# Where SBUF tiles begin: one rule for all of them in place of a table of offsets for the split weights

## The chip, the cores and the metric

The kernel runs on one core of one Trainium2 chip. The time is that of one execution on the device in microseconds (us); three executions of the kernel before gave 3103.0, 3103.5 and 3106.6 us, with a median of 3103.5 us.

## The reference

The reference is a small model in float32 on 256 tokens of width 2048: an RG-LRU/mLSTM layer, an SSD layer, a block that mixes an S5, a gated-linear-attention and a differential-attention branch, and a gated feed-forward block, each with a root-mean-square norm and a residual. Nearly all of its arithmetic is in products of the activations with weight matrices:

```python
def rmsnorm(x, w):
    xf = x.astype(jnp.float32)
    y = xf * lax.rsqrt(jnp.mean(xf * xf, axis=-1, keepdims=True) + EPS)
    return (y * w.astype(jnp.float32)).astype(x.dtype)
...
    u = x @ w_in            # lru_mlstm_layer and ssd_layer: 2048 x 8192 and 2048 x 10304
...
    return y @ w_out        # 4096 x 2048
```

The other weights of that kind are `w_in_2`, `w_out_2`, `ffn_w_up_2` (2048 x 11008), `ffn_w_down_2` and a few smaller ones. The result is wanted in float32, and the matrices are used once each.

## The kernel before

Activations stand with features on the 128 partitions and the 256 tokens along the free axis, two feature blocks to a tile: a tile `x`, `a`, `h` or `b` is 128 x 2 x 256 float32, 2048 bytes in each partition. A weight matrix is cut into blocks of 128 x 128. They come from HBM in one long stream, in the order in which they are used: SP's queue loads eight blocks at a time into a tile `w` (three buffers), and `_split_part` makes of every four blocks (a **part**) two tiles: `wh`, the weights rounded to float32r by ScalarE (L249), and `wl`, the remainder, by VectorE (L250). There are six buffers of each. `ahead` runs this five parts ahead of the products.

`prod` (L280 to L282) multiplies one block with one 128 x 256 activation block in three matmuls: `wh` with the high half of the activations, `wh` with their low half, and `wl` with the high half. They add up in a PSUM tile `pm`. Before each matmul TensorE loads its weights anew, so the stream is a chain of pairs: a weight load (128 columns, 512 bytes in each partition) and a matmul (256 columns, 1024 bytes in each partition). The load for the next matmul runs while the present one streams its activations. The trace has 24,144 such pairs; the program has 8048 blocks, and 3 x 8048 = 24,144. In the main pattern a part gives twelve matmuls, L280, L281, L282 four times.

Everything else (convolutions, scans, norms, gates, the small matmuls of the branches) runs beside the stream on VectorE, ScalarE and GpSimd, or is put into the stream in short pieces by `pump`.

SBUF is given out by pools in the order in which they are opened: constants (`cst`), the weight stream (`wp`: `w`, `wh`, `wl`), activations that live long (`xp`), scratch (`tmp`), and then the pools of each stage. Every pool begins where the one before ends. In the kernel before, the sizes of the small constant tiles so set where all that follows begins. `wpart` gives each `wh` and `wl` tile 96 bytes more than it needs (2144 in place of 2048) and lets the weights begin some bytes into it:

```python
WH_OFF, WL_OFF = (0, 0, 0, 0, 16, 16), (8, 8, 4, 4, 24, 12)
...
    def wpart(self, tag, o):

        t = self.wp.tile([P, SP * P + 24], F32R, name=self.nm(tag), tag=tag, bufs=6)
        return t[:, o // 4:o // 4 + SP * P].rearrange("p (b c) -> p b c", b=SP)
...
        h = self.wpart("wh", WH_OFF[i % 6])
        l = self.wpart("wl", WL_OFF[i % 6])
```

The part's number modulo 6 picks the offset.

Of the kernel before, what the change touches and what calls it, by code (L numbers as in the profile page):

```python
# [9 lines left out]
F32 = mybir.dt.float32  # L10
F32R = mybir.dt.float32r
# [8 lines left out]
P = 128  # L20
T = 256
D = 2048
KD = D // P
EPS = 1e-6
CH = 8

# [4 lines left out]
SP = 4  # L31

WH_OFF, WL_OFF = (0, 0, 0, 0, 16, 16), (8, 8, 4, 4, 24, 12)
HEADS = 4
# [62 lines left out]
NPAR = _o  # L97
# [9 lines left out]
NCON = _o  # L107
# [44 lines left out]
class Builder:  # L152
    def __init__(self, nc, tc, d, dbg, ctx):
        self.nc, self.tc, self.d, self.dbg = nc, tc, d, dbg
        self.ctx = ctx
        pool = lambda **k: ctx.enter_context(tc.tile_pool(**k))
        self.cst = pool(name="cst", bufs=1)
        self.wp = pool(name="wp", bufs=1)
        self.xp = pool(name="xp", bufs=1)
        self.tp = pool(name="tmp", bufs=1)  # L160
        self.pm = pool(name="pm", bufs=1, space=PSUM)
        self.ps = pool(name="ps", bufs=1, space=PSUM)
        self.dr = pool(name="dr", bufs=1, space=DRAM)
        self.uid = 0
        self.side = []

        self.plan = []
        at = {}
        for name, n in _plan():
            assert n % CH == 0, name  # L170
            for _ in range(n // CH):
                self.plan.append((name, at.get(name, 0)))
                at[name] = at.get(name, 0) + 1
        self.w_dma = 0
        self.w_split = 0
        self.w_pos = 0
        self.raw, self.hl = {}, {}
# [10 lines left out]
    def close(self, cm):  # L188
        cm.__exit__(None, None, None)

    def act(self, shape=(P, 2, T), dt=F32, pool=None):
# [44 lines left out]

    def wpart(self, tag, o):

        t = self.wp.tile([P, SP * P + 24], F32R, name=self.nm(tag), tag=tag, bufs=6)
        return t[:, o // 4:o // 4 + SP * P].rearrange("p (b c) -> p b c", b=SP)  # L240

    def _split_part(self, i):
        nc = self.nc
        c, b = divmod(i * SP, CH)
        w = self.raw[c][:, b:b + SP]
        h = self.wpart("wh", WH_OFF[i % 6])
        l = self.wpart("wl", WL_OFF[i % 6])
        for s in [slice(0, SP)] if i else [slice(0, SP // 2), slice(SP // 2, SP)]:
# [191 lines left out]
    def run(self):  # L440
        nc, d = self.nc, self.d
        self.params = self.cst.tile([P, NPAR], F32, name="params")
        self.consts = self.cst.tile([P, NCON], F32, name="consts")

# [72 lines left out]
    def layer_one(self):  # L517
# [14 lines left out]

        cmw = self.cst.tile([P, 80], F32, name="cmw")
        nc.vector.tensor_scalar(cmw, self.par("conv_m_w", 0, 80), 0.5, None, op0=ALU.mult)
# [9 lines left out]

        sp = self.cst.tile([P, 16], F32, name="lru_sp")
        hb = self.cst.tile([P, 32], F32, name="lru_hb")
        lam = self.par("lru_lam", 0, 16)
# [279 lines left out]
    def layer_two(self):  # L827
# [8 lines left out]
        self.st, scm = self.open("ssd")  # L836
        cw = st.tile([P, 240], F32, name="ocw")
        nc.vector.tensor_scalar(cw, self.par("o_conv_w", 0, 240), 0.5, None, op0=ALU.mult)
# [51 lines left out]

        fw = st.tile([P, 16], F32, name="fw")
        nc.vector.tensor_tensor(fw, self.par("final_norm", 0, 16), self.par("norm_mix", 0, 16), op=ALU.mult)
# [617 lines left out]
    def diff(self, qd, kd, vd, oh, ol):  # L1510
# [11 lines left out]
        nc.scalar.dma_start(ali, d["consts2"][:, 384:].rearrange("p (h k) -> p h k", h=4))  # L1522
        lam = self.st.tile([P, 1], F32, name="lam")
        V.tensor_tensor(lam, e[:, 0:1], e[:, 1:2], op=ALU.subtract)
# [37 lines left out]
    def ffn(self):  # L1562
# [5 lines left out]
        self.stage = (st, "a", 34)  # L1568
        gw = st.tile([P, 4, 43], F32, name="gw")
        for k in range(3):  # L1570
# [169 lines left out]
```

## Time and profile before

| | |
|---|---|
| median of three runs | 3103.5 us |
| the profiled execution's own time | 3105.49 us |
| its span, first to last instruction | 3103.7 us |
| TensorE (matmul) busy | 3080.1 us, 99% |
| TensorE weight loads busy | 3029.1 us, 98% |
| VectorE busy | 2301.3 us, 74% |
| ScalarE busy | 1748.7 us, 56% |
| GpSimd busy | 90.5 us, 3% |
| DMA | 556 MB, 179 GB/s on average |
| mean granted TensorE clock | 0.997 of full speed |

A matmul's row in the trace lasts some 282 ns although the next one begins after some 118 ns: matmuls are pipelined. What one costs in the stream is therefore the distance from its start to the next one's start, here called its **pace**. It is read from the timeline (starts of neighbouring rows) or from the windows view (length of a stretch divided by the count of matmuls that lie in it). The timeline shows starts to 0.01 us; the trace holds them in nanoseconds, and means over many matmuls below are taken from those.

### The profile page before, as it was taken

Reading aid. Unit: us, or ns where it says so; the run is one execution under the profiler, and the core shown is the slowest. Engines: PE = TensorE matmul, PEld = TensorE weight load, DVE = VectorE, ACT = ScalarE, POOL = GpSimd, SP = SyncE. Lnnn points to the kernel's source line nnn. Section 1 sums busy time; section 2 is a strip of 40 time slices with the busy share of each in tenths; the row PEclk is TensorE's granted clock in tenths of the full one; section 3 lists DMA queues with packets and bytes.
Section 4 is the critical chain, followed back from the end, with each engine's and each line's share of the span. In section 5 each row is a group of like instructions: output and inputs, shape, how many; then the busy total and the mean of one; then the engine's idle time right before and its main releaser. Section 6 shows DMA issues by size and latency. Waiting matters only on the chain.

```text
span 3103.7 us, 66894 instructions
## 1 busy us (share of the span) xinstructions
PE 3080.1 (99%) x26310; PEld 3029.1 (98%) x26310; DVE 2301.3 (74%) x4693; ACT 1748.7 (56%) x3303; POOL 90.5 (3%) x123
## 2 busy tenths in 40 slices
PE   8999999999999999999999999999999999999998
PEld 8999999999999999999999998999999999999998
DVE  8787766669888876778888786666677777567764
ACT  6666544556666555564555554555555555455554
POOL 1000000010000000020000000000000000000000
PEclk9999999999999999999999999999999999999999
DMA  6565545656565555565454554556556565655654
GB/s 233 182 184 161 178 159 184 186 178 217 185 191 175 168 179 180 193 200 178 153 154 152 165 170 149 160 162 203 186 184 187 184 186 188 185 184 186 188 184 150
DMA packets 153933, 556.30 MB, mean 179 GB/s; under 512 B 17392, under 2 KB 18544, under 8 KB 152592
## 3 DMA queue, kind: packets, MB, share of 16 engines
q1 hardware_dynamic: 148752, 534.89, 54.9%
q0 software_dynamic: 3104, 14.75, 1.3%
q8 instruction: 206, 3.38, 0.4%
q10 hardware_dynamic: 1760, 2.38, 0.2%
q14 instruction: 111, 0.91, 0.1%
HBM read 547.69 MB, written 4.26 MB: 178 GB/s over the span
## 4 chain that ended last, share of the span: by engine, by line
PE 99%; DVE 1%; DMA 0%; ACT 0%; issue 0%; SPq 0%; DVEq 0%
PE pm L280 31%; PE pm L282 31%; PE pm L281 31%; PE ps L1004 1%; PE ps L1306 0%; PE ps L1344 0%; PE ps L1465 0%; PE ps L369 0%; PE ps L1291 0%; PE ps L1236 0%; PE ps L798 0%; PE ps L973 0%; PE ps L682 0%; PE ps L683 0%; DMA w<-w_first 0%; PE ps L1440 0%
## 5 line engine op out<-in xcount | busy, mean ns | idle before, releaser
L249 ACT CAST wh<-w 128x512 fp32r<-128x512 f32 (+1 forms) x2013 | 1239.6, 622 | 1212.6 <-PE pm L281 1028.5
L250 DVE TENSOR_TENSOR wl<-w,wh 128x512 fp32r<-128x512 f32 (+1 forms) x2013 | 1392.5, 698 | 635.8 <-ACT wh L249 611.2
L280 PE MATMUL pm<-x,wh 128*128 128x256 f32 x5504 | 1559.0, 283 | 6.1 <-ACT wh L249 6.1
L282 PE MATMUL pm<-x,wl 128*128 128x256 f32 x5504 | 1553.3, 283 | 3.3 <-DVE q L426 3.1
L281 PE MATMUL pm<-x,wh 128*128 128x256 f32 x5504 | 1549.7, 282 | 0.5 <-DVE x L487 0.4
L280 PEld LDWEIGHTS pm<-x,wh 128*128 128x128 f32 x5504 | 1040.5, 189 | 15.0 <-issue 7.8
L282 PEld LDWEIGHTS pm<-x,wl 128*128 128x128 f32 x5504 | 1039.4, 189 | 7.2 <-DVE q L426 3.3
L281 PEld LDWEIGHTS pm<-x,wh 128*128 128x128 f32 x5504 | 1039.9, 189 | 3.2 <-issue 1.9
L280 PE MATMUL pm<-a,wh 128*128 128x256 f32 x1712 | 483.1, 282 | 0.5 <-ACT wh L249 0.5
L282 PE MATMUL pm<-a,wl 128*128 128x256 f32 x1712 | 483.0, 282 | 0.0
L281 PE MATMUL pm<-a,wh 128*128 128x256 f32 x1712 | 481.9, 282 | 0.3 <-DVE a L333 0.3
L280 PEld LDWEIGHTS pm<-a,wh 128*128 128x128 f32 x1712 | 323.4, 189 | 0.9 <-ACT wh L249 0.7
L281 PEld LDWEIGHTS pm<-a,wh 128*128 128x128 f32 x1712 | 322.6, 188 | 0.6 <-DVE a L333 0.5
L282 PEld LDWEIGHTS pm<-a,wl 128*128 128x128 f32 x1712 | 322.6, 188 | 0.2
L280 PE MATMUL pm<-h,wh 128*128 128x256 f32 x576 | 163.6, 284 | 0.6 <-DVE t L1090 0.6
L281 PE MATMUL pm<-h,wh 128*128 128x256 f32 x576 | 162.5, 282 | 0.0
L282 PE MATMUL pm<-h,wl 128*128 128x256 f32 x576 | 161.8, 281 | 0.0
L280 PEld LDWEIGHTS pm<-h,wh 128*128 128x128 f32 x576 | 108.5, 188 | 4.6 <-issue 3.1
L281 PEld LDWEIGHTS pm<-h,wh 128*128 128x128 f32 x576 | 108.7, 189 | 0.8 <-issue 0.8
L282 PEld LDWEIGHTS pm<-h,wl 128*128 128x128 f32 x576 | 108.5, 189 | 0.0
L417 DVE SCALAR_TENSOR_TENSOR a<-t,ocw,a 128x255 f32<-128x255 f32 (+1 forms) x144 | 64.6, 477 | 20.2 <-ACT a L415 20.1
L282 PE MATMUL pm<-b,wl 128*128 128x256 f32 x256 | 72.1, 282 | 0.0
(430 smaller groups left out, 2411.7 us busy)
## 6 DMA issues: line engine op xcount, KB each, us to landing
w<-w_up SPq DMA_DIRECT2D x172, 512.0 KB, 3.5
w<-w_w_in_u SPq DMA_DIRECT2D x114, 512.0 KB, 3.6
w<-w_o_in SPq DMA_DIRECT2D x98, 512.0 KB, 3.9
w<-w_w_in_g SPq DMA_DIRECT2D x96, 512.0 KB, 3.5
w<-w_down SPq DMA_DIRECT2D x86, 512.0 KB, 3.5
w<-w_e_in_z SPq DMA_DIRECT2D x64, 512.0 KB, 3.5
w<-w_e_out SPq DMA_DIRECT2D x64, 512.0 KB, 3.5
w<-w_o_z SPq DMA_DIRECT2D x64, 512.0 KB, 3.5
```

The lines of the kernel that those rows point to most:

```text
L249: nc.scalar.copy(h[:, s], w[:, s])
L250: nc.vector.tensor_tensor(l[:, s], w[:, s], h[:, s].bitcast(F32), op=ALU.subtract)
L280: nc.tensor.matmul(o, h, xh(k), start=k == 0, stop=False)
L281: nc.tensor.matmul(o, h, xl(k), start=False, stop=False)
L282: nc.tensor.matmul(o, l, xh(k), start=False, stop=k == KT - 1)
L417: nc.vector.scalar_tensor_tensor(dst[:, j:], u[:, :T - j], ws[taps - 1 - j], dst[:, j:], op0=ALU.mult, op1=ALU.add)
L1004: nc.tensor.matmul(o, xdt[s][:, 64 * ee:64 * ee + 64], r, start=s == 0, stop=s == 1, tile_position=(0, 64 * e))
```

## The change

The table of offsets and `wpart` go. `wh` and `wl` become plain tiles of 2048 bytes. A helper `line` rounds the odd-sized tiles (`params`, `consts`, `cmw`, `lru_sp`, `lru_hb`, `ocw`, `fw`, `lam`, `gw`) up to a multiple of 128 bytes, and two small pools of 64 bytes, `gap1` and `gap2`, stand before and behind the weight stream's pool.

```diff
--- before.py
+++ after.py
@@ -22,6 +22,7 @@
 D = 2048
 KD = D // P
 EPS = 1e-6
+LINE = 128
 CH = 8
 
 
@@ -29,8 +30,6 @@
 
 
 SP = 4
-
-WH_OFF, WL_OFF = (0, 0, 0, 0, 16, 16), (8, 8, 4, 4, 24, 12)
 HEADS = 4
 
 L1_ORDER = [("m", 0), ("l", 0), ("m", 1), ("q", 0), ("l", 1), ("l", 2), ("q", 1), ("m", 2), ("l", 3), ("l", 4), ("q", 2), ("m", 3), ("l", 5), ("l", 6), ("q", 3), ("l", 7)]
@@ -155,7 +154,10 @@
         self.ctx = ctx
         pool = lambda **k: ctx.enter_context(tc.tile_pool(**k))
         self.cst = pool(name="cst", bufs=1)
+
+        pool(name="gap1", bufs=1).tile([P, LINE // 8], F32, name="gap1")
         self.wp = pool(name="wp", bufs=1)
+        pool(name="gap2", bufs=1).tile([P, LINE // 8], F32, name="gap2")
         self.xp = pool(name="xp", bufs=1)
         self.tp = pool(name="tmp", bufs=1)
         self.pm = pool(name="pm", bufs=1, space=PSUM)
@@ -188,6 +190,14 @@
     def close(self, cm):
         cm.__exit__(None, None, None)
 
+    def line(self, shape, name, pool):
+
+        n = math.prod(shape[1:])
+        t = pool.tile([P, -(-n // (LINE // 4)) * (LINE // 4)], F32, name=name)[:, 0:n]
+        if len(shape) == 3:
+            t = t.rearrange("p (a b) -> p a b", a=shape[1])
+        return t
+
     def act(self, shape=(P, 2, T), dt=F32, pool=None):
 
         pool, tag, n = pool or self.stage
@@ -234,17 +244,12 @@
             self.nc.sync.dma_start(w[:, s], src[:, s])
         self.raw[i] = w
 
-    def wpart(self, tag, o):
-
-        t = self.wp.tile([P, SP * P + 24], F32R, name=self.nm(tag), tag=tag, bufs=6)
-        return t[:, o // 4:o // 4 + SP * P].rearrange("p (b c) -> p b c", b=SP)
-
     def _split_part(self, i):
         nc = self.nc
         c, b = divmod(i * SP, CH)
         w = self.raw[c][:, b:b + SP]
-        h = self.wpart("wh", WH_OFF[i % 6])
-        l = self.wpart("wl", WL_OFF[i % 6])
+        h = self.wp.tile([P, SP, P], F32R, name=self.nm("wh"), tag="wh", bufs=6)
+        l = self.wp.tile([P, SP, P], F32R, name=self.nm("wl"), tag="wl", bufs=6)
         for s in [slice(0, SP)] if i else [slice(0, SP // 2), slice(SP // 2, SP)]:
             nc.scalar.copy(h[:, s], w[:, s])
             nc.vector.tensor_tensor(l[:, s], w[:, s], h[:, s].bitcast(F32), op=ALU.subtract)
@@ -439,8 +444,8 @@
 
     def run(self):
         nc, d = self.nc, self.d
-        self.params = self.cst.tile([P, NPAR], F32, name="params")
-        self.consts = self.cst.tile([P, NCON], F32, name="consts")
+        self.params = self.line([P, NPAR], "params", self.cst)
+        self.consts = self.line([P, NCON], "consts", self.cst)
 
         st, self.start = self.open("start")
         x0 = st.tile([P, KD + 2 * T], F32, name="x0")
@@ -530,7 +535,7 @@
         nc.scalar.mul(rhalf, rstd, 0.5)
 
 
-        cmw = self.cst.tile([P, 80], F32, name="cmw")
+        cmw = self.line([P, 80], "cmw", self.cst)
         nc.vector.tensor_scalar(cmw, self.par("conv_m_w", 0, 80), 0.5, None, op0=ALU.mult)
         assert POFF["conv_m_b"] == POFF["conv_m_w"] + 64
         self.close(self.start)
@@ -542,8 +547,8 @@
         big = st.tile([P, 384], F32, name="big3")
         nc.scalar.dma_start(big, d["consts2"][:, 0:384])
 
-        sp = self.cst.tile([P, 16], F32, name="lru_sp")
-        hb = self.cst.tile([P, 32], F32, name="lru_hb")
+        sp = self.line([P, 16], "lru_sp", self.cst)
+        hb = self.line([P, 32], "lru_hb", self.cst)
         lam = self.par("lru_lam", 0, 16)
         u, s, q = self.small([P, 16]), self.small([P, 16]), self.small([P, 16])
         nc.scalar.activation(u, lam, AF.Abs)
@@ -834,7 +839,7 @@
         st, cm = self.open("two")
         self.stage = (st, "a", 28)
         self.st, scm = self.open("ssd")
-        cw = st.tile([P, 240], F32, name="ocw")
+        cw = self.line([P, 240], "ocw", st)
         nc.vector.tensor_scalar(cw, self.par("o_conv_w", 0, 240), 0.5, None, op0=ALU.mult)
         assert POFF["o_conv_b"] == POFF["o_conv_w"] + 192
 
@@ -888,7 +893,7 @@
 
 
 
-        fw = st.tile([P, 16], F32, name="fw")
+        fw = self.line([P, 16], "fw", st)
         nc.vector.tensor_tensor(fw, self.par("final_norm", 0, 16), self.par("norm_mix", 0, 16), op=ALU.mult)
         self.acc, self.acc2 = [], []
         self.xh, self.xl = [], []
@@ -1520,7 +1525,7 @@
         nc.scalar.activation(e, p, AF.Exp)
         ali = self.st.tile([P, 4, T], F32, name="alibi")
         nc.scalar.dma_start(ali, d["consts2"][:, 384:].rearrange("p (h k) -> p h k", h=4))
-        lam = self.st.tile([P, 1], F32, name="lam")
+        lam = self.line([P, 1], "lam", self.st)
         V.tensor_tensor(lam, e[:, 0:1], e[:, 1:2], op=ALU.subtract)
         V.tensor_scalar(lam, lam, LAMBDA_INIT, None, op0=ALU.add)
         scale = float(np.float32(128 ** -0.5))
@@ -1566,7 +1571,7 @@
 
         st, cm = self.open("ffn")
         self.stage = (st, "a", 34)
-        gw = st.tile([P, 4, 43], F32, name="gw")
+        gw = self.line([P, 4, 43], "gw", st)
         for k in range(3):
             nc.vector.tensor_scalar(gw[:, k], self.par("ffn_conv_w", 86 * k + 43, 43), 0.5, None, op0=ALU.mult)
         nc.vector.tensor_scalar(gw[:, 3], self.par("ffn_conv_b", 43, 43), 0.5, None, op0=ALU.mult)
```

No instruction is added, removed or moved: on each of the five engines the built program has the same instructions in the same order, with the same waits, and every tile keeps its number of buffers. What differs is where tiles begin. From the two built programs, in bytes within a partition:

| tiles | before | after |
|---|---|---|
| `wh` (6 buffers, with offset) | 0, 16, 32, 48, 64, 80 or 96 past a multiple of 128 | 64 past, all |
| `wl` (6 buffers, with offset) | 4, 8, 12, 36, 40, 68, 88, 104 or 120 past, never a multiple of 16 | 64 past, all |
| `w` | 96 past | 64 past |
| activations that the stream's matmuls read (`x`, `a`, `h`, `b`) | 96 past (87% of the matmuls) or 32 past | 0, all |
| `params`, `consts`, scratch, other stage tiles | 0, 32, 64 or 96 past | 0 |
| the S5 branch's tiles `s5bc` to `s5yx` | 0 | 32 past |

One more quantity is used below. The **distance** is the start of the activations that a matmul reads, less the start of the weights that are loaded meanwhile for the next matmul, modulo 512. (A weight block is 512 bytes and an activation block 1024, so all blocks of one part and one tile pool share a distance.) Before, parts come in 27 pairs of distances, one for `wh` and one for `wl`, which lies 60 to 72 bytes below it, modulo 512. After, both have the same distance in a part: 64 for 68.2% of the stream's matmuls, 192 for 20.7%, 448 for 8.7% and 320 for 2.4%.

## Rows read from the trace of the kernel before

**Rows 1.** The page: busy time, granted clock, and the chain that ended last

```profile
PE 3080.1 (99%) x26310; PEld 3029.1 (98%) x26310; DVE 2301.3 (74%) x4693; ACT 1748.7 (56%) x3303; POOL 90.5 (3%) x123
...
PEclk9999999999999999999999999999999999999999
...
PE 99%; DVE 1%; DMA 0%; ACT 0%; issue 0%; SPq 0%; DVEq 0%
PE pm L280 31%; PE pm L282 31%; PE pm L281 31%; PE ps L1004 1%; PE ps L1306 0%; PE ps L1344 0%; PE ps L1465 0%; PE ps L369 0%; PE ps L1291 0%; PE ps L1236 0%; PE ps L798 0%; PE ps L973 0%; PE ps L682 0%; PE ps L683 0%; DMA w<-w_first 0%; PE ps L1440 0%
```

**Rows 2.** The page's groups: line, tiles, count, busy us, mean ns, idle before

```profile
L249 ACT CAST wh<-w 128x512 fp32r<-128x512 f32 (+1 forms) x2013 | 1239.6, 622 | 1212.6 <-PE pm L281 1028.5
L250 DVE TENSOR_TENSOR wl<-w,wh 128x512 fp32r<-128x512 f32 (+1 forms) x2013 | 1392.5, 698 | 635.8 <-ACT wh L249 611.2
L280 PE MATMUL pm<-x,wh 128*128 128x256 f32 x5504 | 1559.0, 283 | 6.1 <-ACT wh L249 6.1
...
L280 PE MATMUL pm<-a,wh 128*128 128x256 f32 x1712 | 483.1, 282 | 0.5 <-ACT wh L249 0.5
...
L280 PE MATMUL pm<-h,wh 128*128 128x256 f32 x576 | 163.6, 284 | 0.6 <-DVE t L1090 0.6
...
L282 PE MATMUL pm<-b,wl 128*128 128x256 f32 x256 | 72.1, 282 | 0.0
```

**Rows 3.** Windows of uninterrupted stream: stretch, length, PE busy (matmuls), clock, DMA

```profile
2100.00:2140.00 40.00, 40.00 (x335) 1.00 0.65 213
...
2700.00:2960.00 260.00, 260.00 (x2197) 1.00 0.60 187
3020.00:3080.00 60.00, 60.00 (x509) 1.00 0.58 176
```

**Rows 4.** Four transposes of 128 columns in a row: timeline, then durations by line

```profile
732.61 0.60 PE L973 MATMUL ps<-consts,a 128*128 128x128 f32 x4
...
L973 PE MATMUL ps<-consts,a x64: 270/273/276, 732.6 to 1013.2; 128*128 128x128 f32 x64
```

**Rows 5.** Timeline, distance 64 for wh: the first part and the last

```profile
2139.99 0.28 PE L282 MATMUL pm<-h,wl 128*128 128x256 f32 x1
2140.10 0.28 PE L280 MATMUL pm<-h,wh 128*128 128x256 f32 x1
2140.22 0.28 PE L281 MATMUL pm<-h,wh 128*128 128x256 f32 x1
...
2141.40 0.28 PE L282 MATMUL pm<-h,wl 128*128 128x256 f32 x1
...
3081.86 0.28 PE L282 MATMUL pm<-a,wl 128*128 128x256 f32 x1
...
3083.27 0.28 PE L282 MATMUL pm<-a,wl 128*128 128x256 f32 x1
```

**Rows 6.** Timeline, distances 192 and 448 for wh: one part each

```profile
1128.14 0.28 PE L282 MATMUL pm<-a,wl 128*128 128x256 f32 x1
...
1129.56 0.28 PE L282 MATMUL pm<-a,wl 128*128 128x256 f32 x1
...
1996.79 0.28 PE L282 MATMUL pm<-x,wl 128*128 128x256 f32 x1
...
1998.21 0.28 PE L282 MATMUL pm<-x,wl 128*128 128x256 f32 x1
```

**Rows 7.** Timeline, distances 352 for wh and 284 for wl: one part

```profile
37.31 0.28 PE L282 MATMUL pm<-x,wl 128*128 128x256 f32 x1
...
38.77 0.28 PE L282 MATMUL pm<-x,wl 128*128 128x256 f32 x1
```

**Rows 8.** By line: durations in ns (least, median, most) of the two splitting operations

```profile
L249 ACT CAST wh<-w x2013: 388/621/740, 5.1 to 3080.6; 128x512 fp32r<-128x512 f32 x182, 128x256 fp32r<-128x256 f32 x1
...
L250 DVE TENSOR_TENSOR wl<-w,wh x2013: 411/692/1280, 5.5 to 3081.3; 128x512 fp32r<-128x512 f32 x182, 128x256 fp32r<-128x256 f32 x1
```

## The prediction

> **What bounds the kernel now.** The page comes first. TensorE is busy 99% of the span with matmuls and 98% with weight loads, the clock was granted in full in nearly every slice, and 99% of the chain that ended last is TensorE's own work, 93% of it the three lines of the weight stream [rows 1]. So the next question is not who waits for whom but what one matmul of the stream costs. The groups give the count: 5504 + 1712 + 576 + 256 = 8048 matmuls on each of L280, L281 and L282 (a group with the same count stands for each line), 24,144 in all, and almost no idle time before them, 6.1 us at most [rows 2]. The windows give the pace: 40.00 us / 335 = 119.4 ns, 260.00 / 2197 = 118.3, 60.00 / 509 = 117.9 [rows 3]. Over the 23,706 starts in the timeline that follow directly on one another (under 200 ns apart), the mean is 118.6 ns. 24,144 x 118.6 = 2863 us of the 3103.7 us span; the other 240 us are the small matmuls, the start and the end. A change of 1 ns in the pace is worth 24.1 us, 0.8% of the time, and 0.2% (6.2 us, about what a measurement of this kernel can tell from no change) is 0.26 ns.
>
> Is 118.6 ns near a floor? Four transposes of 128 columns take 0.60 us; without the last one's own 273 ns that is (600 - 273) / 3 = 109 ns for each pair of a weight load and a short matmul [rows 4]. The stream's pairs load as many weights and take 9.6 ns more, so up to 24,144 x 9.6 = 232 us could depend on how the two reads of SBUF meet.
>
> **That the pace depends on addresses** can be read from the trace of before, since the old table puts the weights at many distances from the activations. Take a part's twelve matmuls, from the start of the matmul before its first to the start of its last. With distances 352 (wh) and 284 (wl), the part in the rows takes 38.77 - 37.31 = 1.46 us, 121.7 ns each; all 111 such parts have a mean of 121.0 ns and a standard deviation of 0.2 [rows 7]. With distance 64 for wh and 504 or 508 for wl, the first part takes 2141.40 - 2139.99 = 1.41 us and the last 3083.27 - 3081.86 = 1.41 us, 117.5 ns each; all 46 have a mean of 117.9 and a deviation of under 0.2 [rows 5]. So what repeats is the pair of distances, not the stage: the 46 parts lie in three stages and read tiles h, b and a. Of the 1738 undisturbed parts, the means of the 27 pairs lie between 117.4 and 121.0.
>
> The Trainium skill speaks against this: "TensorE: Matmul & The Clock Gate", in Part 2, step 1, says that loading the next weights doesn't take read bandwidth from the running matmul, as there are two read ports, and "SBUF — State Buffer", in Who interferes with whom, says that PE never waits on anyone. By that rule the 121.0 and 117.9 ns should be one number, and the change would be worth nothing. The trace doesn't agree, but the rule has a milder form that is a rival below.
>
> **The change, part by part.**
>
> *Instructions.* None is added, removed or moved, no wait is new, and the number of buffers is the same. So every term but the pace is zero, if durations elsewhere don't follow alignment. For ScalarE's and VectorE's splits I can say so: they write to all of the old offsets, and the medians are 621 and 692 ns [rows 8]; grouped by offset, the means lie within 618 to 625 and 694 to 702 ns, in no order. Should they move by these few ns, ScalarE's idle time before L249 (1212.6 us) and VectorE's before L250 (635.8 us) take it up [rows 2]. The S5 tiles that go from 0 to 32 past a line feed small matmuls only, well under 100 us in all; 1% of that would be under 1 us, and I count it as zero.
>
> *The pace, activations at distance 64 (68.2% of the matmuls).* Two neighbours bound it. One is the whole part with wh at 64: 117.9 ns [rows 5]. In it, wl stands at 504 or 508, not at 64 as after. The other is the pace of single matmuls: a step from a start on L280 to the next on L281, as 2140.10 to 2140.22 in the rows [rows 5], is the only one in which this weight load and the one before it stand at 64, as all do after. The 188 such steps, of which that is the first, have a mean of 116.2 ns, the lowest of 21 distances on that line (all steps to L281 together: 119.0). But their gain is partly given back in the step before, to L280, 119.4 ns, which follows a load of wl at 504 or 508. I take 117.3, two thirds of the way to the whole part, since whole parts repeat much better than single steps.
>
> *The pace, distances 192 and 448.* Whole parts with wh at 192: 13, mean 118.5 (in the rows 1129.56 - 1128.14 = 1.42 us, 118.3 each); with wh at 448: 104, mean 118.9 (1998.21 - 1996.79 = 1.42 us) [rows 6]. For distance 320 (2.4%) 14 parts have 118.4. In all of these wl stands some 70 lower than wh; where it stands after, I have no row, so they are taken as they are.
>
> *The sum.* 0.682 x 117.3 + 0.207 x 118.5 + 0.087 x 118.9 + 0.024 x 118.4 = 117.7 ns, 0.9 less than 118.6. 24,144 x 0.9 ns = 21.7 us. The profiled execution took 3105.5 us, so 3083.8; it was 2.0 us above the median of the runs, so 3082 us.
>
> *What no row shows.* All activations of the stream begin 32 or 96 past a multiple of 128 in the kernel before, never 0 or 64. That only the distance counts is borne out for a shift of 64 (distance 64: 117.8 ns from the 96s, with wl at 504, and 118.0 from the 32s, with wl at 508; 448: 118.9 and 118.9; but 256 with 184: 119.8 and 120.3), not for one of 32. Nor does any row have wl at a multiple of 16: steps to L282 with their odd offsets have a mean of 118.1, against 118.8 and 119.0 to L280 and L281, so losing the offsets could cost up to 0.9 ns on a third of the matmuls, 7 us. Bounds: all at 116.2 gives -2.4 ns, -58 us, 3046; all as slow as the slowest pair gives +2.4 ns, +58 us, 3162; the floor gives -232 us.
>
> **The rivals.**
>
> *No change.* The pace's excess could be a cost of the pair itself, with the addresses only moving it from one step to the next. For it: 26 of the 27 pairs lie within 117.4 and 119.9, so most of the 9.6 ns is there at any distance. Against it: 121.0 repeats 111 times. Then 3103 us, within 6 us. By the skill's two sentences above it would be this.
>
> *Slower.* With weights and activations on the same grid of 64 bytes, and wl no longer shifted, each load meets the stream at the same phase every time. The rows to price it: the 1474 steps with a distance of 64 modulo 128, as all have after, have a mean of 119.4 ns, 0.8 over the whole, much of it from the steps to L280 at 448, 122.1 ns. 24,144 x 0.8 = 19 us: 3123. It decides if the steps to L280 stay as slow as 119.4 and those to L282 join them, that is from a pace of 118.9.
>
> *Much faster.* The excess could come from what all pairs of before have in common: activations that begin 32 bytes off a multiple of 64, so that the two reads cross their lines at different times. If half of the 9.6 ns went, it would be 116 us: 2988. For it speaks only that no distance of before takes away the excess; against it, weights that begin at a multiple of 64 (0 or 64 past, 4278 steps, 119.2 ns) are no faster than others. It decides from a pace under 116.
>
> **How the numbers follow.** The forecast, faster by 6 to 80 us: 0.50. Much faster: 0.12. No change: 0.17. Slower: 0.21. So faster by over 0.2% is 0.62, within it 0.17, slower 0.21. The time is that of the likeliest case, 3082 us. The range runs from 3025, beyond all steps at 116.2 and some way to the much faster case, which is left out with most of its chance, to 3122, where the slower case stands; some 0.2 lies outside, half on each side.
>
> **What the profile after would show.** The same counts and the same order; TensorE at 99% and the clock full. Windows of uninterrupted stream: 260 us should hold some 2209 matmuls in place of 2197. Stretches whose activations are x tiles should be the fastest, with 117.3 ns and little spread between parts, since all buffers now stand alike; steps to L281 should stay near 116. The durations of L249 and L250 should not move. The prediction is wrong in its main step if parts on x tiles run at 118.5 or more, which means that a distance's pace doesn't carry over to activations that begin at a multiple of 128; and it is wrong in size if they run under 116.

## The result, and the profile after

The changed kernel takes **3062.2 us** (median of 4 runs, 3060.3 to 3065.8) against 3104.6 us: ratio 0.987, 95% interval 0.985 to 0.988, so 1.3% or 42 us faster. The profiled execution took 3060.3 us with a span of 3058.5 us.

First the page of the changed kernel (busy time, clock, and the chain that ended last, as in [rows 1]). The stream's lines L280 to L282 are now L285 to L287, the splits L249 and L250 are L254 and L255.

```profile
PE 3034.5 (99%) x26310; PEld 2984.9 (98%) x26310; DVE 2296.5 (75%) x4693; ACT 1747.9 (57%) x3303; POOL 90.8 (3%) x123
...
PEclk9999999999999999999999999999999999999999
...
PE 98%; DVE 1%; DMA 0%; ACT 0%; issue 0%; SPq 0%; DVEq 0%
```

The counts are as before, the clock as well, and the chain is still TensorE's own work. What is gone is busy time of TensorE: 3080.1 - 3034.5 = 45.6 us, as much as the span lost (45.2 us). Next the page's groups (count | busy us, mean ns | idle before), which answer [rows 2].

```profile
L254 ACT CAST wh<-w 128x512 fp32r<-128x512 f32 (+1 forms) x2013 | 1239.3, 622 | 1172.7 <-PE pm L286 868.1
L255 DVE TENSOR_TENSOR wl<-w,wh 128x512 fp32r<-128x512 f32 (+1 forms) x2013 | 1389.3, 696 | 603.0 <-ACT wh L254 583.3
L285 PE MATMUL pm<-x,wh 128*128 128x256 f32 x5504 | 1545.0, 281 | 6.1 <-ACT wh L254 6.1
...
L285 PE MATMUL pm<-a,wh 128*128 128x256 f32 x1712 | 477.0, 279 | 0.5 <-ACT wh L254 0.5
```

The splits keep their 622 and 696 ns (622 and 698 before), and TensorE's waits are the same 6.1 and 0.5 us. Only the matmuls changed: 281 for 283 ns on x, 279 for 282 on a. Over the 23,710 starts that follow directly on one another the mean pace is 116.79 ns, against 118.60. 24,144 x 1.81 ns = 43.7 us, nearly all of the 45.2 us that the span lost.

The windows of TensorE (stretch, length, busy time with matmuls, clock, DMA share, GB/s) show that this mean is made of two levels. A window also counts the matmuls that hang over its ends, so its pace is (length + 0.28 us) / count. A part is called undisturbed when its twelve steps, and the one behind them, all took under 200 ns.

```profile
467.00:487.00 20.00, 20.00 (x178) 1.00 0.63 194
495.00:515.00 20.00, 20.00 (x172) 1.00 0.64 188
682.00:698.00 16.00, 16.00 (x144) 1.00 0.63 183
702.00:718.00 16.00, 16.00 (x138) 1.00 0.77 280
2400.00:2500.00 100.00, 100.00 (x852) 1.00 0.60 186
2700.00:2960.00 260.00, 260.00 (x2220) 1.00 0.60 187
```

The first pair lies in one unbroken run of the stream: a tiles (distance 192) at 20.28 / 178 = 113.9 ns, then x tiles (64) at 117.9. The second pair is x tiles at the same distance 64, in two runs with a piece of a branch between them: 16.28 / 144 = 113.1 ns and 16.28 / 138 = 118.0. Of the 1738 undisturbed parts of the whole trace, 23% lie at 113.3 ns and nearly all others at 117.8; only 0.1% have a mean between 114.6 and 117. In shares below, a part counts to the nearer of the two levels. In the kernel before no part was at 113.3, and its 27 pairs of distances had means of their own. A pair didn't fix its pace even there: parts at 16 (`wh`) and 468 (`wl`) took 117.6 ns behind a part at 432 and 360 (116 parts), and 118.7 behind one at 336 and 264 (79). By distance, with all weights standing alike:

| distance | parts | mean ns | deviation | share at the 113.3 level | predicted ns |
|---|---|---|---|---|---|
| 64 (x) | 1172 | 117.46 | 1.17 | 7% | 117.3 |
| 192 | 349 | 115.98 | 2.15 | 40% | 118.5 |
| 448 (FFN-down) | 171 | 113.34 | 0.09 | all | 118.9 |
| 320 | 46 | 117.87 | 0.14 | none | 118.4 |

The timeline of the changed kernel (start, duration, line, tiles) at the change from x (64) to a (448) in the FFN shows one such switch:

```profile
2573.09 0.28 PE L285 MATMUL pm<-a,wh 128*128 128x256 f32 x1
...
2573.44 0.28 PE L285 MATMUL pm<-a,wh 128*128 128x256 f32 x1
...
2574.46 0.28 PE L285 MATMUL pm<-a,wh 128*128 128x256 f32 x1
```

The first three steps take 350 ns, 117 each; the next nine take 1.02 us, 113 each. From there the stream stays at 113.3 for as long as the a tiles last.

### The profile page after: what moved, and what is told of

It reads as the page before. It is cut to its first block, busy times and chain, and to the rows that moved or that the text cites. A ratio compares the mean times of both kernels' runs of the same rounds, so it can differ in the third digit from the quotient of the medians.

```text
span 3058.5 us, 66894 instructions
## 1 busy us (share of the span) xinstructions
PE 3034.5 (99%) x26310; PEld 2984.9 (98%) x26310; DVE 2296.5 (75%) x4693; ACT 1747.9 (57%) x3303; POOL 90.8 (3%) x123
## 3 DMA queue, kind: packets, MB, share of 16 engines
q10 hardware_dynamic: 1760, 2.38, 0.3%
## 4 chain that ended last, share of the span: by engine, by line
PE 98%; DVE 1%; DMA 0%; issue 0%; ACT 0%; SPq 0%; DVEq 0%
PE pm L285 31%; PE pm L286 31%; PE pm L287 31%; PE ps L1009 1%; PE ps L1311 0%; PE ps L1349 0%; PE ps L1470 0%; PE ps L374 0%; PE ps L1296 0%; PE ps L1241 0%; PE ps L803 0%; PE ps L978 0%; PE ps L687 0%; PE ps L688 0%; DVE wl L255 0%; PE ps L1445 0%
## 5 line engine op out<-in xcount | busy, mean ns | idle before, releaser
L254 ACT CAST wh<-w 128x512 fp32r<-128x512 f32 (+1 forms) x2013 | 1239.3, 622 | 1172.7 <-PE pm L286 868.1
L255 DVE TENSOR_TENSOR wl<-w,wh 128x512 fp32r<-128x512 f32 (+1 forms) x2013 | 1389.3, 696 | 603.0 <-ACT wh L254 583.3
L285 PE MATMUL pm<-x,wh 128*128 128x256 f32 x5504 | 1545.0, 281 | 6.1 <-ACT wh L254 6.1
L286 PE MATMUL pm<-x,wh 128*128 128x256 f32 x5504 | 1541.0, 280 | 0.5 <-DVE x L492 0.4
L287 PE MATMUL pm<-x,wl 128*128 128x256 f32 x5504 | 1538.2, 280 | 3.2 <-DVE q L431 3.0
L285 PEld LDWEIGHTS pm<-x,wh 128*128 128x128 f32 x5504 | 1034.6, 188 | 15.0 <-issue 7.8
L287 PEld LDWEIGHTS pm<-x,wl 128*128 128x128 f32 x5504 | 1032.9, 188 | 7.1 <-DVE wl L255 4.5
L286 PEld LDWEIGHTS pm<-x,wh 128*128 128x128 f32 x5504 | 1033.9, 188 | 3.2 <-issue 1.9
L285 PE MATMUL pm<-a,wh 128*128 128x256 f32 x1712 | 477.0, 279 | 0.5 <-ACT wh L254 0.5
L287 PE MATMUL pm<-a,wl 128*128 128x256 f32 x1712 | 476.3, 278 | 0.0
L286 PE MATMUL pm<-a,wh 128*128 128x256 f32 x1712 | 475.8, 278 | 0.4 <-DVE a L338 0.4
L286 PEld LDWEIGHTS pm<-a,wh 128*128 128x128 f32 x1712 | 322.5, 188 | 0.8 <-DVE a L338 0.6
L287 PEld LDWEIGHTS pm<-a,wl 128*128 128x128 f32 x1712 | 322.3, 188 | 0.2
L285 PEld LDWEIGHTS pm<-a,wh 128*128 128x128 f32 x1712 | 321.5, 188 | 0.9 <-ACT wh L254 0.7
L285 PE MATMUL pm<-h,wh 128*128 128x256 f32 x576 | 162.2, 282 | 0.8 <-DVE t L1095 0.8
L286 PE MATMUL pm<-h,wh 128*128 128x256 f32 x576 | 160.8, 279 | 0.0
L287 PE MATMUL pm<-h,wl 128*128 128x256 f32 x576 | 160.6, 279 | 0.0
L285 PEld LDWEIGHTS pm<-h,wh 128*128 128x128 f32 x576 | 108.1, 188 | 4.8 <-issue 3.1
L286 PEld LDWEIGHTS pm<-h,wh 128*128 128x128 f32 x576 | 108.1, 188 | 0.8 <-issue 0.8
L287 PEld LDWEIGHTS pm<-h,wl 128*128 128x128 f32 x576 | 108.8, 189 | 0.0
L287 PE MATMUL pm<-b,wl 128*128 128x256 f32 x256 | 71.9, 281 | 0.0
```

The lines of the kernel that those rows point to most:

```text
L254: nc.scalar.copy(h[:, s], w[:, s])
L255: nc.vector.tensor_tensor(l[:, s], w[:, s], h[:, s].bitcast(F32), op=ALU.subtract)
L285: nc.tensor.matmul(o, h, xh(k), start=k == 0, stop=False)
L286: nc.tensor.matmul(o, h, xl(k), start=False, stop=False)
L287: nc.tensor.matmul(o, l, xh(k), start=False, stop=k == KT - 1)
```

## The experiments

Two questions: is it the distance alone, or the place on the grid as well; and where do the two levels come from. All ratios below are to the kernel before, whose median was 3105.5 to 3106.5 us beside these runs. "Fast level" in the expectations means 113.3 ns, "slow" 117.8.

### Everything 32 bytes on, after and before

```diff
-        pool(name="gap1", bufs=1).tile([P, LINE // 8], F32, name="gap1")
+        pool(name="gap1", bufs=1).tile([P, LINE // 8 + 8], F32, name="gap1")
```

> The changed kernel with the pad ahead of the weights 32 bytes longer: weights begin 96 bytes past a multiple of 128 instead of 64, activations 32 past instead of 0, and every distance between an activation and the next weights is as in the changed kernel. Theory 'only the distance counts': mean pace 116.8 ns with the same parts fast and slow, time within 6 us of 3062. Rival 'the start on a multiple of 64 counts as well' (the kernel before had its activations 32 or 96 past 128 and a mean pace of 118.6): the pace goes back most of the way, to between 118 and 118.6 ns, time 3090 to 3105.

Measured: 3062.2 us, ratio 0.986 (0.985 to 0.987), mean pace 116.86 ns. The four means of the table above return as 117.55, 115.98, 113.34 and 117.87. The window of 260 us holds 2219 matmuls for 2220:

```profile
2700.00:2960.00 260.00, 260.00 (x2219) 1.00 0.60 187
```

The same on the kernel before:

```diff
+        pool(name="gap1", bufs=1).tile([P, 8], F32, name="gap1")
         self.wp = pool(name="wp", bufs=1)
```

> The kernel before with 32 bytes of pad ahead of its weight pool: all its weights with their offset table and all its activations move on by 32 bytes, so that activations begin on a multiple of 64 and every distance stays what it was before. Theory 'only the distance counts': mean pace 118.6 ns, time within 6 us of 3104. Rival 'activations off a multiple of 64 cost something' (the prediction's third rival): pace under 117.5 ns, time under 3080.

Measured: 3105.0 us, ratio 1.000 (0.999 to 1.001), pace 118.60, and 2198 matmuls in the same window for 2197 [rows 3]:

```profile
2700.00:2960.00 260.00, 260.00 (x2198) 1.00 0.60 186
```

A start on or off a multiple of 64 is worth nothing here: of the addresses, only distances count.

### The table gone alone, and the rounding alone

The offset table gone, but no pads and no rounding:

```diff
-        pool(name="gap1", bufs=1).tile([P, LINE // 8], F32, name="gap1")
...
-        pool(name="gap2", bufs=1).tile([P, LINE // 8], F32, name="gap2")
...
+        t = pool.tile(list(shape), F32, name=name)
```

> The changed kernel without its two pads and without the rounding up of the small tiles: what is left of the change is that the offset table of the weights is gone and all weight tiles are alike, 96 bytes past a multiple of 128, with activations 96 or 32 past. Distances are 0 for the x tiles, 64, 128 and 320 for the rest. Theory 'distance sets the pace': the x parts take one pace with little spread; no part of either kernel stood at distance 0, so its level is open between the two levels of the changed kernel, 113.3 and 117.8 ns, or above the pace before, 118.6, if standing at the same place costs most; the time is then 2985 to 3062, or over 3104. Rival 'what helped was the start on multiples of 128 and the offset table had no part in it': the pace stays at 118.6 ns, time near 3104.

Measured: **3125.3 us**, ratio 1.006 (1.005 to 1.008): slower. The x parts stand at distance 0 and take 119.97 ns, with a deviation of 0.15; at 128 it is 118.71. A window of x products in the FFN, of this kernel:

```profile
2400.00:2500.00 100.00, 100.00 (x836) 1.00 0.59 184
```

836 matmuls where the changed kernel has 852: 119.95 ns against 117.7. And the rounding alone, with the old table of offsets and no pads:

```diff
-        pool(name="gap1", bufs=1).tile([P, LINE // 8], F32, name="gap1")
-        pool(name="gap2", bufs=1).tile([P, LINE // 8], F32, name="gap2")
...
-        h = self.wp.tile([P, SP, P], F32R, name=self.nm("wh"), tag="wh", bufs=6)
+        h = self.wpart("wh", WH_OFF[i % 6])
```

> The changed kernel with its two pads gone and the old table of offsets for the weights put back: what is left of the change is that every other tile begins at a multiple of 128. The x parts then stand at the same distances as in the kernel before (16 and 468, 128 and 56, 256 and 188, and so on), but at addresses 0 past 128 instead of 96. Theory 'distances alone': pace 118.4 to 118.8 ns, time 3098 to 3110. Rival 'the start at multiples of 128 is worth something of its own': pace under 118, time under 3090.

Measured: 3103.6 us, ratio 1.000 (0.999 to 1.001). The pairs of distances keep their means from one kernel to the other: 352 with 284, 121.03 (121.04 in the kernel before moved by 32 bytes); 256 with 188, 117.76 (117.73). So neither has a gain of its own, and the pads count: behind plain weight tiles x stands at 0, and the 64 bytes of `gap2` put it at 64. By tiles, 18 of the 43 us that the steps lost come from x (118.59 to 117.45 ns over some 16,200 steps), 20 from a (118.63 to 114.73 over 5080) and the rest from h and b. Pads with plain tiles but without the rounding were not run.

### All x tiles at 448

```diff
-        pool(name="gap2", bufs=1).tile([P, LINE // 8], F32, name="gap2")
+        pool(name="gap2", bufs=1).tile([P, LINE // 8 + 96], F32, name="gap2")
```

> The changed kernel with the pad behind the weights 384 bytes longer, so that every activation tile moves on by 384 bytes and nothing else: the x tiles (68% of the stream) go from distance 64 to 448, the a tiles of the FFN from 448 to 320, those that stood at 192 to 64. Theory 'the distance sets the pace, and 448 is the good one' (parts at 448 ran at 113.3 ns in the changed kernel, all of them, parts at 64 at 117.5): the x parts run at 113.3 to 113.6 ns, the mean pace is about 114.6 ns instead of 116.8, and the time is about 52 us under the changed kernel's 3062, near 3010. Rival 'the parts at 448 were fast because of their stage, the FFN-down products, not because of the distance': the x parts stay at 117.5 ns, the FFN-down parts, now at 320, stay at 113.3, and the time stays within 10 us of 3062.

Measured: 3040.8 us, ratio 0.979 (0.978 to 0.981): 21 us under the changed kernel, where the theory wanted 52. The x parts have a mean of 114.88 ns with a deviation of 2.1: 66% lie at 113.3, the others at 117.8. The FFN-down products, now at 320, all lie at 117.8, so it was not their stage. A window of this kernel shows FFN x products at (100.28 / 885 =) 113.3 ns:

```profile
2400.00:2500.00 100.00, 100.00 (x885) 1.00 0.63 195
```

So a distance doesn't fix the level, it opens one. I then put the a, h and b tiles at 448 as well, with five pads (three are shown):

```diff
         self.st = st
+        st.tile([P, 96], F32, name="gap3")
...
         self.stage = (st, "a", 28)
+        st.tile([P, 96], F32, name="gap4")
...
         self.stage = (st, "a", 34)
+        st.tile([P, 32], F32, name="gap7")
```

> The kernel of the first experiment with five more pads, one at the head of each stage's tiles, so that every activation tile of the stream stands at distance 448. Theory 'the distance sets which levels are open to the stream (at 448 both 113.3 and 117.8 ns), and a break sets which of them an unbroken run takes': x parts about as before, 65% of them fast, the other 32% of the stream falls from 117.8 to the same mix, 114.9 ns: 0.32 x 2.9 = 0.9 ns or 22 us less than 3041, near 3019; every unbroken run lies on one level from its first part to its last, the long one of the FFN (6,097 steps) as well. At best, all parts at 113.3, it is 2981. Rival 'the change of distance between the parts of x and of a is what brings the stream back to the fast level' (in the FFN each return from 320 to 448 was fast): without it the runs of the ssd stage and the FFN lie on the slow level, and the time is above 3041, up to 3075.

Measured: 3048.4 us, ratio 0.982 (0.981 to 0.983): slower than with x alone at 448, as the rival said. The same window of this kernel, at the same distance as in the last one:

```profile
2400.00:2500.00 100.00, 100.00 (x851) 1.00 0.60 188
```

It holds 851 matmuls for 885. In this kernel no unbroken run holds both levels; the one of 6,097 steps in the FFN lies at 117.8 from end to end, and so does the one of 1,893 before it. With x alone at 448 these two runs began at 113.3 and came back to it behind every undisturbed part at 64 or 320 (8 of 8). The change of distance alone doesn't do that: in other runs of the same kernel, which had been slow at 64 from their first part, 6 of the 8 first changes from 64 to 448 led to 117.8. Where a run had been at 448 before, it took the level that it had had there (9 of 9, all fast); in the changed kernel so did the returns from 64 to 192 (3 fast, 10 slow). So the starts of the two long runs, rather than the changes, seem to make the difference, though no run sets them apart.

What the kernels show is that **at one distance a run keeps its level**: of 4859 pairs of neighbouring parts at one distance with no step of 200 ns or more, in the changed kernel and these two, none goes from one level to the other. A stretch at another distance can change it: at 192, with x alone at 448, one return fell from 113.3 to 117.8.

What a break does is partly seen in the first step behind it, which takes 200 to 230 ns or some 306 (runs of 30 steps or more). Where it took 220 to 224 ns, 13 of 17 runs went on at 113.3 in the changed kernel, 22 of 25 with x at 448, 29 of 31 with all at 448, and 12 of 18 in the changed kernel moved by 32 bytes; where it took 225 to 230 ns, none of 22, 14, 8 and 21. Two such starts in the timeline of the changed kernel, ahead of the windows at 682 and 702 us:

```profile
680.11 0.36 PE L285 MATMUL pm<-x,wh 128*128 128x256 f32 x1
680.32 0.28 PE L286 MATMUL pm<-x,wh 128*128 128x256 f32 x1
...
700.06 0.39 PE L285 MATMUL pm<-x,wh 128*128 128x256 f32 x1
700.29 0.28 PE L286 MATMUL pm<-x,wh 128*128 128x256 f32 x1
```

The second takes 228 ns and stays at 118. The first takes 201 ns, a length behind which either level follows (in this kernel 13 of the 73 starts under 220 ns went on at 113.3).

### A distance that changes with every part

Weight buffers 64 bytes further on from one to the next, h and l alike (the line for `l` and the pads are left out):

```diff
-        h = self.wp.tile([P, SP, P], F32R, name=self.nm("wh"), tag="wh", bufs=6)
+        h = self.wp.tile([P, SP * P + 16], F32R, name=self.nm("wh"), tag="wh", bufs=6)[:, 0:SP * P].rearrange("p (b c) -> p b c", b=SP)
...
```

> The changed kernel with the six weight buffers 64 bytes further on from one to the next (h and l tile of a buffer alike): consecutive parts of the x products stand at distances 448, 384, 320, 256, 192 and 128, those of the rest at the other multiples of 64. It is a measurement of the distances by themselves. Theory 'odd multiples of 64 are good, even ones bad' (0 took 119.97 ns, 128 took 118.7; 64, 192, 320 and 448 took 113.3 to 117.9): the parts at 256 and 384 lie over 118.5 ns, those at 192, 320 and 448 at 117.8 or under; time 3060 to 3110. Rival 'every distance but 0 can be fast, 128 was only never caught by its breaks': parts at 256 and 384 reach 113.3 too, somewhere.

Measured: 3057.5 us, ratio 0.985 (0.983 to 0.986). At 64, 192, 320 and 448 between 84% and 99% of the parts are at the 113.3 level (means 114.6, 113.7, 114.1, 114.4), also at 64 and 320, which hardly ever were in the changed kernel. At 0, 128, 256 and 384 none is (119.5, 118.1, 119.5, 118.3). The rival fell. With steps of 32 bytes:

```diff
-        h = self.wp.tile([P, SP * P + 16], F32R, name=self.nm("wh"), tag="wh", bufs=6)[:, 0:SP * P].rearrange("p (b c) -> p b c", b=SP)
+        h = self.wp.tile([P, SP * P + 8], F32R, name=self.nm("wh"), tag="wh", bufs=6)[:, 0:SP * P].rearrange("p (b c) -> p b c", b=SP)
...
```

> The same with steps of 32 bytes: consecutive parts of the x products stand at 480, 448, 416, 384, 352 and 320, the rest at the other multiples of 32. Theory 'only odd multiples of 64 are open to the fast level': parts at 32, 96, 160 and so on stay at 117.4 ns or more, as all distances of the kernel before did; time 3075 to 3110. Rival 'what kept the kernel before from the fast level was the change of distance from part to part, not the distance': then here, too, no part is fast, those at 448 and 320 included, and in the run with steps of 64 none either.

Measured: 3092.2 us, ratio 0.996 (0.994 to 0.997), pace 118.14. No part at an odd multiple of 32 is at the 113.3 level (116.7 ns at 288, 117.0 at 32, up to 120.0 at 352), though two of these means lie under the theory's 117.4. Of the odd multiples of 64 almost none is at 64, 192 or 320 (at most 3%), while at 448 72% are: all 78 behind a part at 384, all 34 behind one at 96, 54 of 95 behind one at 416, none of 18 behind one at 32. So what a part comes from matters, and the rival fell. That suggested one buffer of six as a lever (from here on all activations are padded to 448 as above; `wq` is a second pool behind `wp`, with a pad between them, which is left out):

```diff
+        wp, n = (self.wq, 1) if i % 6 == 5 else (self.wp, 5)
+        h = wp.tile([P, SP, P], F32R, name=self.nm("wh"), tag="wh", bufs=n)
...
```

> The kernel with all activations at 448, in which one of the six weight buffers (h and l tile) stands 64 bytes further on, so that every sixth part of the stream is at distance 384 and the other five at 448. Theory 'a step from an even to an odd multiple of 64 brings the stream to the fast level': parts at 448 behind one at 384 took 114.4 ns in the run with steps of 64, and the next ones should stay at 113.3; with 118.1 ns for the sixth part the mean pace is (4 x 113.4 + 114.4 + 118.1) / 6 = 114.3 ns, time near 3000. Rival 'it was the change in every part that kept those runs fast': the level still follows the breaks, the pace lies over 116 ns and the time over 3040.

Measured: **3011.3 us**, ratio 0.970 (0.968 to 0.972). All 279 parts at 448 behind one at 384 are nearer to 113.3 than to 117.8, and the parts behind them stay there; the parts at 384 cost 118.19. The mean is 114.69, 0.4 above the estimate: 8% of the parts at 448 still lie at 117.8, those that come ahead of the first 384 of their run. And with two odd multiples in turn:

```diff
-        wp, n = (self.wq, 1) if i % 6 == 5 else (self.wp, 5)
+        wp, n = (self.wq, 3) if i % 2 else (self.wp, 3)
...
```

> The same with three of the six weight buffers 128 bytes further on, in turn with the other three: parts at 448 and 320 in turn, both odd multiples of 64. Theory 'it takes a part at an even multiple to bring a slow stream to the fast level; between odd ones a stream keeps the level that it has': about half the stream is fast, by the breaks as in the kernel with all at 448, the pace lies between 115 and 116.5 ns, time 3020 to 3050. Rival 'any change of distance into 448 brings it to the fast level' (from 320 to 448 it did in the FFN): parts at 448 are all fast, and if those at 320 behind them keep that (they did in the run with steps of 64, not in the first experiment), the pace is 113.5 ns and the time near 2985.

Measured: **2993.8 us**, ratio 0.964 (0.963 to 0.965). My theory fell, the rival's time was off by 9 us. Of 78 parts at 448 that follow a part at 320 of the slow level, 95% are at 113.3; of the 320s behind a 448 at 113.3 (746) all stay there. 94% of all parts are now at that level.

### The turn within each triple

```diff
         h = self.wp.tile([P, SP, P], F32R, name=self.nm("wh"), tag="wh", bufs=6)
-        l = self.wp.tile([P, SP, P], F32R, name=self.nm("wl"), tag="wl", bufs=6)
+        l = self.wq.tile([P, SP, P], F32R, name=self.nm("wl"), tag="wl", bufs=6)
...
```

> The kernel with 448 and 320 in turn, the turn now within each triple of matmuls: all h tiles of the weights at distance 448, all l tiles at 320, so that the distance goes 448, 448, 320 from step to step. Theory 'each step from 320 to 448 draws the stream to the fast level': it is fast within a few steps of every break, pace 113.3 to 113.8 ns, time 2980 to 2996. Rival 'a level needs a stretch at one distance to settle, and what switches it is the start of a new part': the pace does not lock, as in the kernel before, whose h and l tiles stood at different distances too, and lies between 116 and 119 ns, time 3045 to 3115.

Measured: **2985.9 us**, ratio 0.962 (0.960 to 0.963): 3.8% under the kernel before, 2.5% under the changed one (76 us; by the paces 24,144 x (116.79 - 113.55) = 78). 99.7% of the parts are on the 113.3 level, with a mean of 113.37. Over the 125 runs of 30 steps or more, the mean of the first step after the long one is 118.9 ns, of the tenth 113.5, and from the twelfth on one step of 21,423 is over 115 (126 ns, the last of its run). The page of this kernel, and its windows:

```profile
PE 2957.4 (99%) x26310; PEld 2907.9 (97%) x26310; DVE 2289.9 (77%) x4693; ACT 1744.4 (58%) x3303; POOL 90.2 (3%) x123
```

```profile
2100.00:2140.00 40.00, 40.00 (x356) 1.00 0.62 193
2400.00:2500.00 100.00, 100.00 (x885) 1.00 0.63 195
2700.00:2960.00 260.00, 260.00 (x2297) 1.00 0.62 192
```

The 260 us hold 2297 matmuls, 77 more than in the changed kernel, and the three stretches now have one pace, 113.1 to 113.3 ns; TensorE is still what bounds the kernel. Last, whether any turn of 128 bytes does this, without the pads of the stages:

```diff
+        pool(name="gap8", bufs=1).tile([P, 32], F32, name="gap8")
+        self.wq = pool(name="wq", bufs=1)
-        pool(name="gap2", bufs=1).tile([P, LINE // 8], F32, name="gap2")
+        pool(name="gap2", bufs=1).tile([P, LINE // 8 + 96], F32, name="gap2")
...
-        l = self.wp.tile([P, SP, P], F32R, name=self.nm("wl"), tag="wl", bufs=6)
+        l = self.wq.tile([P, SP, P], F32R, name=self.nm("wl"), tag="wl", bufs=6)
```

> The changed kernel with one edit, without any pad of the stages: its l tiles stand 128 bytes further on than its h tiles (a pad between the two sets; the pad behind is longer, so that the activations keep their distance to the h tiles). The x products then go 64, 64, 448 from step to step, those at 192 in the changed kernel 192, 192, 64, the FFN-down products 448, 448, 320. Theory 'it is the turn of 128 bytes within each triple that draws the stream to the fast level, whichever odd multiples of 64 it is between': pace 113.4 to 114 ns everywhere, time 2985 to 3000. Rival 'it is 448 behind 320 alone': only the FFN-down products (8.5% of the stream) are fast in all their parts, as they were already; x products at 64 stay near 117.5, time 3045 to 3065.

Measured: 3044.6 us, ratio 0.980 (0.979 to 0.982), between the two. With wh at 192 and wl at 64 all 349 parts are at 113.3 (40% with both at 192), and so are all 171 with 448 and 320. With 320 and 192 none of 46 is (118.70), and with 64 and 448, the x products, 34%: the others take 118.9. So this kernel too has two levels at one pair of distances:

```profile
2400.00:2500.00 100.00, 100.00 (x885) 1.00 0.60 194
2800.00:2900.00 100.00, 100.00 (x843) 1.00 0.58 185
```

Both are x products of the FFN, at 113.3 and 119.0 ns. So a turn of 128 bytes isn't enough; of four pairs, the two that draw the stream to 113.3 are 448/320 and 192/64, which differ by 256 from one another. Why these, no run shows.

## Why the prediction was right or wrong

**The forecast of a gain held, at half its size.** It was 3082 us, some 21 us less; measured are 42 us less, within the range of 3025 to 3122.

**What bounds the kernel: right.** The whole change lies in the pace of L285 to L287; outside the direct steps the stream took 271.9 us before and 269.7 after.

**That the pace goes with the pair of distances: half right.** That of the addresses only distances count is shown by the two shifts of 32 bytes (pace unmoved within 0.1 ns) and by the rounding alone, and the worry that an activation at a multiple of 128 might behave in another way fell with them. But a pair doesn't fix the pace. After the change one distance has two levels, and which of them a run takes goes with its start and with what it comes from. The trace of before could have told: 16 with 468 took 117.6 or 118.7 ns, by the part ahead. Its windows were read without the matmul that hangs over the end, too: 119.4, 118.3 and 117.9 ns should be 120.2, 118.5 and 118.4; the sum doesn't use them.

**The term for x, 117.3 ns: right on average** (117.46, worth 0.682 x 0.16 x 24.1 = 3 us the other way), wrong in kind: "little spread" was forecast, and there are two levels, 93% at 117.8 and 7% at 113.3. That the mean came out is luck: neither level was in the forecast, and the two thirds of the way that I took between 116.2 and 117.9 had no mechanism behind it. Steps to L286 did not stay near 116; they have 117.57 at distance 64, and the other two lines 117.46 and 117.31.

**The terms for 192 and 448 failed.** The step is the sentence that these "are taken as they are" because no row had wl at wh's distance. With wl there, 192 fell from 118.5 to 115.98 (0.207 x 2.5 x 24.1 = 12.6 us) and 448 from 118.9 to 113.34 (0.087 x 5.6 x 24.1 = 11.7 us). With the 3 us of x that is the missing 21 us. A pace of a *pair* of distances was carried over to another pair, though the same text had noted that what repeats is the pair. The warning stood in [rows 6]: such parts are the only evidence for 29% of the stream, and all of them have wl some 70 bytes off. How large the gain is also hangs on how runs start: 40% of the parts at 192 were at 113.3, none of them in the run of 1,893 steps and all in that of 1,760, and no row of before could say that.

**No instruction moved, the splits unmoved: right** (622 and 696 ns). The 260 us window holds 2220, not 2209.

**The rivals.** *No change* fell: the same instructions in the same order run at 119.43 ns with the plain tiles and at 113.55 with h at 448 and l at 320, 140 us apart. The Trainium skill ("TensorE: Matmul & The Clock Gate", Part 2, step 1) says that loading the next weights takes no read bandwidth from the running matmul. These two paces don't agree with it as it stands, since only where weights and activations lie differs; how addresses come to matter inside the chip, no run shows. *Slower* came near a price that was measured (3123 us against 3125), but at another distance, with x at 0. Its mechanism, that one phase for every load costs, fell: in the changed kernel every load of a part meets the stream at one distance, and it is faster. What kept x from 0 is the pad `gap2`. *Much faster* named the wrong cause, activations 32 bytes off a multiple of 64 (3105.0 against 3105.8 us when they are put on one), but its size was there to be had: 2988 us by its sum, 2985.9 us by the fastest kernel, with h at 448 and l at 320.

**What stays open:** what in the chip sets the two levels, what decides which of them a run takes (a first step of 225 to 230 ns never led to 113.3 at equal distances, others led to either), which pairs draw a stream in, and why the floor of 109 ns from the transposes [rows 4] was not reached at any distance (no part in any kernel has a mean under 113.2).

## What to carry to other kernels

In a stream that TensorE bounds, read the start-to-start pace of matmuls by part, and look at its histogram before its mean: two sharp levels meant here that part of the stream missed a better state which the layout leaves open. The start of the activations less that of the weights loaded beside them, modulo 512 bytes, is then a thing to choose. It cost pads of 64 to 448 bytes here, while rounding the other tiles by itself was worth nothing (3103.6 us). Price a layout only from rows with the same distances for both weight tiles and the same part ahead, and where there are none, widen the range instead of carrying the nearest mean over.

## What the runs showed of the hardware

At one granted clock (1.00 in every window above), the same pair of a weight load of 128 columns and a matmul of 256 columns took from 113.3 to 121.0 ns, by where the two operands lie in SBUF. With h and l at one distance of 64, 192 or 448 bytes there are two levels, 113.3 and 117.8 ns, and with all at 448 every unbroken run kept the one it started on, for up to 6,097 steps and 718 us. Changing the distance within each triple of matmuls, 448 for h and 320 for l, brought every run of 30 steps or more to the lower level within twelve steps, and that was the fastest layout found here, 2985.9 us.
